# One DMA queue in a fixed order for the loads and stores of a weighted token copy

## The chip, the cores and the metric

The kernel runs on one core of a Trainium2 chip. The metric is the device time of that core in microseconds, as a median over runs. The profile is one execution recorded by the hardware profiler; its span, from the first to the last instruction, is about 2 us shorter than the device time.

## The reference

Every token vector of 512 floats is repeated k = 2 times, once for each of its two experts, and each copy is multiplied by that expert's weight. The expert indices are an input but are not used.

```
x:       (16, 1024, 512)  float32      33.55 MB
weights: (16, 1024, 2)    float32       0.13 MB
x_expanded = x[:, :, np.newaxis, :].repeat(k, axis=2)
out = x_expanded * weights[..., np.newaxis]     # (16, 1024, 2, 512)  67.11 MB
```

One multiplication for each float written: 33.69 MB are read and 67.11 MB are written.

## The kernel before, in words

The 16,384 tokens are laid over the 128 partitions, 128 consecutive tokens to a partition (A_TOTAL = 128). In both memory layouts one partition's share is contiguous, so a tile of 16 tokens is one run of 32 KB per partition, and so is an output tile of 8 tokens with two copies each. Every such transfer is 4096 KB.

The outer loop (L47) runs over 8 input tiles of TX = 16 tokens. It takes a buffer of x_pool, which has two, and loads the tile with a DMA issued from the Scalar engine (L49). The inner loop (L52) makes two output tiles of TO = 8 tokens from it, in buffers of o_pool, which has four. For each token and each k, VectorE multiplies 128x512 floats by a per-partition weight (L59), 16 instructions to an output tile and 32 to an input tile. A DMA issued from the Sync engine stores the output tile (L67). The weights are loaded once at the start from the Sync engine (L45). The two pools together take 2 x 32 KB + 4 x 32 KB = 192 KB of each partition.

The order of the work follows from three things. Each engine runs its own instructions in the order of the program. DMAs of the Sync engine go into one queue (q1 in the profile) and those of the Scalar engine into another (q10); both queues are served by the same 16 DMA engines. And the framework inserts the waits that the buffers need: a multiply waits until its input tile has landed and until the store that last used its output buffer has landed; a store waits for its 16 multiplies; a load waits for the 32 multiplies that read the buffer before. So the Scalar engine issues a load as soon as a buffer is free, whatever the stores are doing, and loads and stores share the DMA engines as they come.

Of the kernel before, what the change touches and what calls it, by code (L numbers as in the profile page):

```python
# [1 line left out]

# [4 lines left out]


@with_exitstack
def kernel(  # L10
    ctx: ExitStack,
    tc: tile.TileContext,
    x: bass.AP,
    expert_indices: bass.AP,
    expert_weights: bass.AP,
    out: bass.AP,
):
    nc = tc.nc

    batch, seq, hidden = x.shape  # L20
    k = expert_weights.shape[-1]
    P = nc.NUM_PARTITIONS
    ntok = batch * seq
    assert ntok % P == 0
    A_TOTAL = ntok // P

    xr = x.rearrange("b s h -> (b s) h").rearrange("(p a) h -> p (a h)", a=A_TOTAL)
    outr = out.rearrange("b s k h -> (b s) (k h)").rearrange(
        "(p a) n -> p (a n)", a=A_TOTAL
    )  # L30
    wr = expert_weights.rearrange("b s k -> (b s) k").rearrange(
        "(p a) k -> p (a k)", a=A_TOTAL
    )
    f32 = mybir.dt.float32
    row = k * hidden

    TX = 16
    TO = 8

    w_pool = ctx.enter_context(tc.tile_pool(name="w_pool", bufs=1))  # L40
    x_pool = ctx.enter_context(tc.tile_pool(name="x_pool", bufs=2))
    o_pool = ctx.enter_context(tc.tile_pool(name="o_pool", bufs=4))

    w_tile = w_pool.tile([P, A_TOTAL * k], f32)
    nc.sync.dma_start(out=w_tile, in_=wr)  # L45

    for i in range(A_TOTAL // TX):  # L47
        x_tile = x_pool.tile([P, TX * hidden], f32)
        nc.scalar.dma_start(  # L49
            out=x_tile, in_=xr[:, i * TX * hidden : (i + 1) * TX * hidden]  # L50
        )
        for j in range(TX // TO):  # L52
            o_tile = o_pool.tile([P, TO * row], f32)
            for t in range(TO):
                at = (j * TO + t) * hidden
                for kk in range(k):
                    c = (i * TX + j * TO + t) * k + kk
                    o = t * row + kk * hidden
                    nc.vector.tensor_scalar(  # L59
                        out=o_tile[:, o : o + hidden],  # L60
                        in0=x_tile[:, at : at + hidden],
                        scalar1=w_tile[:, c : c + 1],
                        scalar2=None,
                        op0=mybir.AluOpType.mult,
                    )
            first = (i * TX + j * TO) * row
            nc.sync.dma_start(out=outr[:, first : first + TO * row], in_=o_tile)  # L67


# [1 line left out]
_INS = ['x', 'expert_indices', 'expert_weights']  # L71
_OUTS = [((16, 1024, 2, 512), 'float32')]


# [23 lines left out]
```

## Time and profile before

| what | value |
|---|---|
| device time, median of 3 runs | 241.06 us (240.87 to 241.54) |
| span of the profiled execution | 238.8 us |
| VectorE busy | 102.5 us (43%), 256 multiplies |
| bytes moved | 100.81 MB, mean 422 GB/s |
| stores: 16 of 4096 KB | 44.9 us from issue to landing (median) |
| loads: 8 of 4096 KB | 23.9 us from issue to landing (median) |

How to read it: time from issue to landing includes the time in which a transfer stands in line behind others, so 44.9 us is no measure of the transfer itself. The share of DMA busy time is a mean over the 16 engines; in short windows it can exceed 1, since a packet is put to the window by its recorded times. Multiplies overlap a little, so that their mean duration (480 ns) is longer than the distance from one to the next (about 400 ns).

### The profile page before, as it was taken

The page shows a single profiled execution, that of the slowest core. Times are in us where ns is not written, and L with a number is a line of the kernel's source. Part 1 is how long each engine was busy: PE and PEld are TensorE (multiplying, and loading weights), DVE is VectorE, ACT ScalarE, POOL GpSimd, SP SyncE. Part 2 cuts the span into 40 slices and gives each one's busy share as a digit, 9 for nine tenths or more (in the row PEclk, how much of TensorE's full clock was granted, in tenths as well). Part 3 has the DMA queues.
Part 4 walks back from the last instruction along what each step waited for, and adds up shares of the span by engine and source line. Part 5 has one row for each costly group of instructions (what it writes and reads, how often), then busy time and mean ns, then how long its engine had stood idle before and what let it go on. Part 6 is the DMA issues. An engine that isn't in the chain of part 4 may idle for free.

```text
span 238.8 us, 358 instructions
## 1 busy us (share of the span) xinstructions
DVE 102.5 (43%) x256; POOL 0.2 (0%) x4
## 2 busy tenths in 40 slices
DVE  0079994059701904682054910739008486400000
POOL 0000000000000000000000000000000000000000
DMA  7999999999999999999999999999999999999994
GB/s 277 447 439 417 434 380 417 439 439 439 423 423 428 439 423 412 439 439 439 439 439 434 434 439 439 412 435 428 428 423 434 434 439 439 439 439 434 434 439 214
DMA packets 3602, 100.81 MB, mean 422 GB/s; under 512 B 400, under 2 KB 528, under 8 KB 528
## 3 DMA queue, kind: packets, MB, share of 16 engines
q1 hardware_dynamic: 2448, 67.24, 65.4%
q10 hardware_dynamic: 1152, 33.55, 33.2%
q14 instruction: 2, 0.02, 0.0%
HBM read 33.69 MB, written 67.11 MB: 422 GB/s over the span
## 4 chain that ended last, share of the span: by engine, by line
DMA 62%; DVE 18%; another core or an unknown queue 5%; DVEq 0%; issue 0%
DMA out_dram<-o_tile 57%; DVE o_tile L59 18%; DMA x_tile<-in_x_dram 5%; DVEq L93 0%; DVEq L59 0%
## 5 line engine op out<-in xcount | busy, mean ns | idle before, releaser
L59 DVE TENSOR_SCALAR o_tile<-x_tile,w_tile 128x512 f32<-128x512 f32 x256 | 102.5, 480 | 103.3 <-DMA out_dram<-o_tile 74.1
L82 POOL MEMSET const-bfloat16-1.0<- 128x1 bf16 x1 | 0.1, 101 | 0.0
L82 POOL MEMSET const-uint8-127<- 128x1 uint8 x1 | 0.1, 101 | 0.0
L82 POOL MEMSET const-float32-0.0<- 128x1 f32 x1 | 0.1, 98 | 0.2 <-issue 0.2
L82 POOL MEMSET const-float32-1.0<- 128x1 f32 x1 | 0.1, 98 | 0.0
## 6 DMA issues: line engine op xcount, KB each, us to landing
out_dram<-o_tile SPq DMA_DIRECT2D x16, 4096.0 KB, 44.9
x_tile<-in_x_dram ACTq DMA_DIRECT2D x8, 4096.0 KB, 23.9
w_tile<-in_expert_weights_dram SPq DMA_DIRECT2D x1, 128.0 KB, 10.1
```

What stands on the lines that cost most here:

```text
L59: nc.vector.tensor_scalar(out=o_tile[:, o : o + hidden], in0=x_tile[:, at : at + hidden], scalar1=w_tile[:, c : c + 1], scalar2=None, op0= ...
L82: nc = _bacc.Bacc("TRN2", target_bir_lowering=False, num_devices=1)
```

## The change

All big transfers go through the Sync engine's queue in a fixed order. Two input tiles are loaded first; then each round stores the two output tiles of tile i and after that loads tile i+2. The weights go to the Scalar engine's queue. Tiles, pools and multiplies stay as they were. The aim is that loads and stores don't share the DMA engines as chance has it, but in an order in which a load can't get ahead of, or slow down, the stores that free output buffers.

```
-    nc.sync.dma_start(out=w_tile, in_=wr)
+    nc.scalar.dma_start(out=w_tile, in_=wr)

-    for i in range(A_TOTAL // TX):
-        x_tile = x_pool.tile([P, TX * hidden], f32)
-        nc.scalar.dma_start(
-            out=x_tile, in_=xr[:, i * TX * hidden : (i + 1) * TX * hidden]
+    x_tiles = {}
+
+    def load(i):
+        x_tiles[i] = x_pool.tile([P, TX * hidden], f32, name="x_tile")
+        nc.sync.dma_start(
+            out=x_tiles[i], in_=xr[:, i * TX * hidden : (i + 1) * TX * hidden]
         )
+
+    load(0)
+    load(1)
+    for i in range(n_tiles):
+        x_tile = x_tiles.pop(i)
         for j in range(TX // TO):
...
             first = (i * TX + j * TO) * row
             nc.sync.dma_start(out=outr[:, first : first + TO * row], in_=o_tile)
+        if i + 2 < n_tiles:
+            load(i + 2)
```

More of the change, by code (lines that the diff above doesn't have):

```diff
@@ L38 @@
     TO = 8
+    n_tiles = A_TOTAL // TX
     w_pool = ctx.enter_context(tc.tile_pool(name="w_pool", bufs=1))
```

## The prediction

> **What bounds the kernel now.** I read the page's busy shares first, then the DMA queues, then a table of stretches, then the waits.
>
> The first view is the page's top: busy time, and the span in 40 slices.
>
> ```profile
> DVE 102.5 (43%) x256; POOL 0.2 (0%) x4
> DMA  7999999999999999999999999999999999999994
> GB/s 277 447 439 417 434 380 417 439 439 439 423 423 428 439 423 412 439 439 439 439 439 434 434 439 439 412 435 428 428 423 434 434 439 439 439 439 434 434 439 214
> q1 hardware_dynamic: 2448, 67.24, 65.4%
> q10 hardware_dynamic: 1152, 33.55, 33.2%
> ```
>
> The only computing engine works 43% of the span. The DMA row is 9 in every slice but the first and the last. The two queues, stores on q1 and loads on q10, add up to 98.6% of 16 engines' span. So the DMA engines are the bound, and what they don't fill is a head and a tail.
>
> The second view cuts the span where the mix of traffic changes. Columns: stretch, its length, DVE busy, POOL busy, clock, DMA share, GB/s.
>
> ```profile
> 0.00:2.00 2.00, 0.00 (x0) 0.20 (x4) 1.00 0.09 11
> 2.00:20.00 18.00, 6.69 (x17) 0.00 (x0) 1.00 1.03 438
> 20.00:50.00 30.00, 18.74 (x48) 0.00 (x0) 1.00 1.01 419
> 50.00:180.00 130.00, 58.02 (x145) 0.00 (x0) 1.00 1.00 431
> 180.00:235.00 55.00, 19.07 (x48) 0.00 (x0) 1.00 1.00 433
> 235.00:238.80 3.80, 0.00 (x0) 0.00 (x0) 1.00 0.30 129
> ```
>
> 2 to 20 us holds almost only loads, 180 to 235 us only stores (the queue rows of those stretches give 101.4% to q10 and 100.2% to q1). Between them both queues are at work. The DMA share is 1 throughout: the change can only gain by a higher rate at full DMA, by a shorter head or by a shorter tail. The rates are 438 (loads), 433 (stores) and 419 and 431 (both).
>
> The third view is who waits for whom.
>
> ```profile
> DVE o_tile L59 <- DMA out_dram<-o_tile: 74.1, 10, 12.9
> DVE o_tile L59 <- DMA x_tile<-in_x_dram: 25.3, 2, 13.3
> ```
>
> VectorE waits 74.1 us for stores to free one of the four output buffers. That looks like a stall to be cured, and the chain of work puts 57% of the span on stores. But while VectorE waits the DMA engines are full, so these waits cost nothing by themselves.
>
> **What the Trainium skill says.** (1) "DMA: Bandwidth & Descriptors", section "Issuing engines are not separate DMA queues": transfers issued from Sync and Scalar run on the same 16 engines, and several issuers save only issue time. The trace agrees: the two queues together reach 431 GB/s, stores alone 433. Issue time is small here (332 ns a store, 366 ns a load, 24 of them). (2) The same page, "Queues, rings and completion order": an engine takes turns between the queues that have work, at packet granularity, and within one queue takes descriptors in ring order. The trace agrees roughly: from 135 to 145 us each queue has 48.5% to 48.6%. (3) The same page, "Two DMAs through the same engine are not ordered": within a queue descriptors start in order but are pipelined. Stores alone show it: transfer follows transfer on one queue at 433 GB/s with no dent. (4) "Perfetto Trace Analysis", section "DMA Optimizations", advises the opposite of this change: inputs on one issuing engine, outputs on another, for more dynamic spread. No run here shows that the spread is worth anything when the engines are full.
>
> **The change part by part.**
>
> *The weights move to the Scalar queue, the first load to Sync.* Both were issued within 0.01 us of each other (0.72 and 0.73 us) and still are. One 128 KB and one 4096 KB transfer share the engines at the start as before. Cost 0.
>
> *What must be ready when.* All 24 big transfers now run in the order load 0, load 1, then (store 2k, store 2k+1, load k+2) six times, then four stores. A transfer is 4096 KB = 4.19 MB; at 433 GB/s it takes 9.7 us. A multiply is issued every 6.42/16 = 0.40 us, so a half tile (16) takes 6.4 us and a tile 12.8 us. Load 0 landed at 13.3 us by the first multiply, so store 0 may go at 19.8 us, as it does now; load 1 keeps the engines until about 22. Store 1 is ready at 26.3 and has its turn at about 32. Load 2 waits for tile 0's multiplies (26.1) and has its turn at about 41. Stores 2 and 3 are ready at 32.6 and 38.9, wanted at 51 and 61. From then on the rule is this: tile i+2 is multiplied in the 12.8 us after its load lands, and in that time the queue still holds two stores and a load, 3 x 9.7 = 29 us of work. Its four-deep output pool is no hindrance, as stores 2i and 2i+1 precede load i+2 in the queue and have landed when it does. At the end load 7 is followed by stores 12 and 13, 19.4 us, and store 14 needs 6.4. The tightest place is store 0, with 2 us in hand. So I expect no idle DMA anywhere.
>
> *The added waits.* A load now sits on Sync behind two stores and may hold the stores behind it. It waits for the multiplies of the tile two before, and the store just ahead of it has waited for the last of these already. So it adds no wait. The output stores behind it are wanted 10 to 30 us later. Cost 0.
>
> *What is left is the rate.* Head and tail stay: the bytes sum to 7.88 + 12.56 + 56.08 + 23.79 MB in 233 us and 0.49 MB after (1.1 us at 433), so the stream takes 234.1 us and head and tail 238.8 - 234.1 = 4.7 us. In the new order each engine sees long runs of one direction. Two ways to price that. If everything after 20 us runs at the store rate of 433, the 12.56 MB of 20 to 50 us take 29.0 us in place of 30, and the 56.08 MB of 50 to 180 us take 129.5 in place of 130: 1.5 us saved. If loads also keep their 438, the first stretch (4.82 MB loads, 7.73 MB stores) takes 11.0 + 17.9 = 28.9 us and the second (20.97 and 35.10 MB) 47.9 + 81.1 = 129.0: 1.1 + 1.0 = 2.1 us saved. I take the middle, 1.8 us.
>
> *The unknown: a change of direction within one queue.* The trace of before has none. There are 13 (load to store seven times, store to load six times). Lower bound: 0, since with both queues at work an engine changes direction at nearly every 1.2 us packet and still gives 431. Upper bound: a full start-up each time. The page "DMA: Bandwidth & Descriptors", section "Latency and other measured facts", gives about 0.6 us to the first byte on this path; 13 x 0.6 = 7.8 us as an estimate. I take 0, because stores follow each other on one queue without a dent.
>
> Sum: 241.06 - 1.8 = 239.2 us.
>
> **The rivals.**
>
> A, the forecast: the mixed stretches rise to the rate of unmixed ones; 239.2 us, between 238.9 and 239.6.
>
> B, no difference: 419 to 438 is scatter of the engines and not of the mix. For it: five-microsecond windows of stores alone go from 419 to 446, and the 130 us of mixed traffic lie only 0.5% under stores alone. The low 20 to 50 us stretch would then be a start-up matter that comes again. Time 240.5 to 241.5.
>
> C, slower: each change of direction in the one queue drains the engine, because there is no second queue with work to fill the gap. For it: the trace has never shown the case, and today a second queue covers whatever gap there is. Against it: transfers on one queue already join without a gap. At 0.3 us each it costs 13 x 0.3 = 3.9 us, less 1.8 us gained: 243.2 us; at the upper bound 247.1.
>
> D, a larger gain: long runs of one direction are better for the memory than the trace can show, and all runs at what loads alone had from 5 to 20 us, (444 + 446 + 433)/3 = 441. 100.81 MB / 441 GB/s = 228.6 us in place of 234.1: 5.5 us saved, 235.5 us. Against it: stores alone have 55 us to show such a rate and stay at 433.
>
> **How the numbers follow.** A 0.55, B 0.20, C 0.17, D 0.08. The time is A's. The range goes down to 237.0, half way to D and a bit over, since loads at 441 would bring nearly that, and up to 241.7, which takes in B and a small C; what is left out is most of C and most of D, about 0.2. Faster by over 0.3% (under 240.3): A and D, 0.63. Within 0.3%: B, 0.20. Slower: C, 0.17.
>
> **What the profile after would show.** Right: DMA digit 9 through all slices but the ends; one queue with about 98% of 16 engines; no stretch of 30 us under 430 GB/s, the one from 20 to 50 us above all; VectorE's waits now put down to loads, in six gaps of about 16 us (29.1 less 12.8), none of which costs anything. Wrong: digits of 7 or 8 that come back every 10 to 20 us, at the seams of loads and stores, for C; the same 419 from 20 to 50 us for B; 440 and over throughout for D. A DMA gap at 20 to 26 us would say that store 0 or 1 came too late for its turn.

## The result and the profile after

The changed kernel takes 244.87 us (244.36 to 245.54, 6 runs) against 241.08 us for the kernel before on the same chip: a ratio of 1.015, 95% interval 1.0121 to 1.0178. It is slower by 1.5%, and the forecast was 239.2 us. On a second chip, beside other kernels below, the ratio was 1.0089 (1.0058 to 1.012): there the changed kernel took much the same time, 245.12 us, and the kernel before took longer, 242.87 us. The kernel before was profiled only once, on the first chip, in an execution of 240.5 us.

The top of the page after, in the same lines as were shown of before:

```profile
DVE 102.0 (42%) x256; POOL 0.2 (0%) x4
DMA  6999999999999999999999999999999999999992
GB/s 276 433 434 426 431 432 410 404 372 437 431 431 426 372 431 431 431 426 415 431 431 431 431 420 427 442 431 431 426 431 431 431 431 431 431 437 431 437 431 108
q1 hardware_dynamic: 3456, 100.66, 97.6%
q10 hardware_dynamic: 144, 0.13, 0.2%
```

Between its ends the DMA row is as full as before, on one queue now. So the DMA engines don't wait for work. But the row of rates has dents (410, 404, 372, then 372 again, 415) that come back at a distance of about five slices, some 30 us, and grow shallower. The same stretches as before, columns as there:

```profile
20.00:50.00 30.00, 18.88 (x48) 0.00 (x0) 1.00 1.01 418
50.00:180.00 130.00, 56.21 (x142) 0.00 (x0) 1.00 1.00 424
180.00:235.00 55.00, 20.33 (x52) 0.00 (x0) 1.00 1.00 431
235.00:243.20 8.20, 0.00 (x0) 0.00 (x0) 1.00 0.46 200
```

The long middle fell from 431 to 424 GB/s at a DMA share of 1.00, which alone is 2.1 us. After 235 us there are 8.2 us in place of 3.8; that is no longer tail of itself, since all that was lost before comes out behind a fixed cut. A busy share of 1 with a lower rate says that the packets themselves take longer. To see which, here are stretches cut at the mean times at which the trace has one transfer end and the next begin: the store before load 2, load 2, two stores, load 3, two stores, load 4.

```profile
32.20:42.20 10.00, 6.67 (x17) 0.00 (x0) 1.00 1.01 419
42.20:53.20 11.00, 0.00 (x0) 0.00 (x0) 1.00 0.99 381
53.20:72.60 19.40, 12.76 (x32) 0.00 (x0) 1.00 1.00 431
72.60:83.40 10.80, 0.00 (x0) 0.00 (x0) 1.00 0.99 382
83.40:102.80 19.40, 12.76 (x32) 0.00 (x0) 1.00 1.00 432
102.80:112.80 10.00, 0.00 (x0) 0.00 (x0) 1.00 1.02 426
```

Loads 2 and 3 take 11.0 and 10.8 us, a store 9.7. The trace keeps every packet's duration, and they tell it best. A 32 KB packet takes 1213 ns in nearly all cases, in either direction and in both kernels: that is 27 GB/s an engine and 432 GB/s for 16. Call what a packet takes beyond that its stretch. The trace doesn't name the engine of a packet, but in most places a packet starts 3 to 4 ns before another one ends, and linked in this way the packets form 16 chains, taken here as the 16 engines. Mean duration in ns of the eight packets that each engine moves for a transfer, in order:

```
changed kernel  store 1  1213 1213 1213 1213 1213 1213 1236 1501
                load 2   1295 1470 1353 1318 1213 1213 1544 1583
                store 2  1213 1213 1213 1213 1213 1213 1213 1213
                store 3  1213 1213 1213 1213 1213 1213 1214 1247
                load 3   1229 1339 1246 1334 1213 1213 1689 1583
                store 4  1213 1213 1213 1213 1213 1213 1213 1213
                load 7   1213 1213 1213 1213 1213 1213 1225 1213
```

The stretch sits where the direction changes: in the last packet of the store ahead of a load, in the first four packets of the load and in its last two. The middle of the load and the stores behind it are at the minimum. It fades: the change from store 1 to load 2 costs 1.6 us, and load 7 has next to none.

In the kernel before each chain has 192 packets, eight for each of the 24 transfers, and so it is in the changed kernel, but for a few that can't be told apart, though the engines end 4 us apart there. So no engine takes over work from a late one. The time is then the minimum, plus the mean stretch, plus how much later than the mean the slowest engine ends. What is left after taking off both is the same within 0.3 us in these three profiles, and most of the rest of this document uses that sum:

```
                          mean stretch   slowest over mean   span    span less both
before                       1.66             1.03           238.8       236.1
changed                      4.25             2.86           243.2       236.1
changed, second chip         3.63             2.99           242.5       235.9
```

So of the 4.4 us between the two spans 2.6 are stretch and 1.8 are more uneven ends (the engines finish their last store 4.3 us apart, before 1.7). This compares one profile with one profile.

### The profile page after: what moved, and what is told of

It is laid out like the page before. It is cut to its first block, busy times and chain, and to the rows that moved or that the text cites. A ratio compares the mean times of both kernels' runs of the same rounds, so it can differ in the third digit from the quotient of the medians.

```text
span 243.2 us, 350 instructions
## 1 busy us (share of the span) xinstructions
DVE 102.0 (42%) x256; POOL 0.2 (0%) x4
## 4 chain that ended last, share of the span: by engine, by line
DMA 65%; DVE 22%; SPq 1%; issue 0%; DVEq 0%
DMA x_tile<-in_x_dram 60%; DVE o_tile L68 22%; DMA w_tile<-in_expert_weights_dram 5%; SPq L76 1%; DVEq L104 0%; DVEq L68 0%; SPq L52 0%
```

## The experiments

**Fewer changes of direction.** Four stores, then two loads: 7 changes in place of 13.

```
-        if i + 2 < n_tiles:
-            load(i + 2)
+        if i % 2 == 1 and i + 1 < n_tiles:
+            load(i + 1)
+            load(i + 2)
```

> One queue, but four stores and then two loads, so that the queue changes direction 7 times and not 13; all tiles as in the changed kernel. Theory (a change of direction costs, as all 16 engines make it at about the same time; in the changed kernel the loads and the packets at the seams took 3.9 us more than their minimum in the mean over the engines, and the engines ended 4.3 us apart): about 7/13 of the loss, 242 to 243 us. Rival 1 (one queue costs something by itself, whatever the order): 244.9 us again. Rival 2 (loads are slow when nothing but loads runs on all engines): 244.9 us or more, the load steps again 10 to 11 us against 9.7.

Measured: 242.02 us, 0.9971 (0.9952 to 0.999) of the kernel before. Since this was another chip than that of the first result, it was run again beside the changed kernel.

> Four stores then two loads, on the same chip as the changed kernel. Theory: 0.985 to 0.992 times the changed kernel, level with the kernel before, about 2.4 us of stretch. Rival (the chip of the earlier set was another, and the order makes no difference): the same as the changed kernel within 0.3%.

> The changed kernel again, beside the others of this set on one chip. Theory and rivals alike: 1.012 to 1.018 times the kernel before, and in the trace about 4 us of packets longer than their minimum in the mean over the engines, most of it at the ends of stores, and in loads, of the first 120 us.

Measured: pairs 242.89 us, 1.0002 (0.9981 to 1.0023) of the kernel before; changed 245.12 us, 1.0089 (1.0058 to 1.012). So pairs take 0.991 of the changed kernel and are level with the kernel before, as the theory had it. Two parts of the expectations missed: the changed kernel came out under its 1.012 to 1.018, and pairs had 3.3 us of stretch in this run, not 2.4. The stretches of the first pairs run: two stores, the store before load 2, load 2, load 3, two stores.

```profile
32.00:51.40 19.40, 6.97 (x18) 0.00 (x0) 1.00 1.00 432
51.40:61.30 9.90, 0.00 (x0) 0.00 (x0) 1.00 0.99 414
61.30:71.50 10.20, 0.00 (x0) 0.00 (x0) 1.00 0.99 414
71.50:81.20 9.70, 8.10 (x21) 0.00 (x0) 1.00 1.00 432
81.20:100.60 19.40, 17.33 (x44) 0.00 (x0) 1.00 1.01 434
```

Load 3 follows load 2 with nothing but loads on all engines and takes 9.7 us: loads as such are not slow (rival 2 falls), and nor is one queue as such (rival 1 falls). The three changes from stores to loads stretch packets by 0.68, 0.77 and 0.55 us; those from loads to stores by 0.08 the first time and by 0.00 the three later times. The ends are 1.5 us apart.

**More changes, smaller transfers.** Half and quarter size, buffers doubled and quadrupled.

```
-    TX = 16
-    TO = 8
+    TX = 8       # quarters: 4
+    TO = 4       # quarters: 2
+    NB = 4       # quarters: 8; loads ahead, bufs=NB and bufs=2 * NB
```

> One queue, two stores then one load, all transfers half as large (2 MB, 16 KB a partition) with twice the buffers, so 26 or so changes of direction. Theory, if each change costs the same: twice the loss, near 249 us; if the loss fades as the engines drift apart, 245 to 247. Rival 1 (the queue by itself): 244.9. Rival 2 (loads alone are slow): 244.9, as the bytes loaded are the same.

> As the kernel with halves, with transfers of 1 MB (8 KB a partition), four times the changes of direction. Theory, each change at the same cost: near 256 us; if a change costs only while some buffering in the DMA engine lasts, less, since the mix then comes close to that of two queues, which took turns packet by packet: 241 to 247. Rivals 1 and 2: 244.9.

Measured: 246.22 us, 1.0152 (1.0101 to 1.0202), and 248.0 us, 1.0222 (1.0178 to 1.0265). The mean stretch was 4.29 and 2.41 us, the ends 4.6 and 5.8 us apart. So the cost does not go with the number of changes: half the stretch of halves comes before 40 us, and it fades from there. The minimum grew: a 16 KB packet takes 611 ns and an 8 KB packet 309. Records of neighbours overlap by 3 to 4 ns, so what counts is the distance from one start to the next, 607 and 306 ns against 1209 for 32 KB; over all packets that is about 1.0 and 2.9 us more. With quarters the slowest engine also ended 4.4 us after the mean (2.9 in the changed kernel). Both together put them above the 241 to 247 us expected of a fading cost, although they have less stretch. The expectation that each change costs the same is refuted; "fades as the engines drift apart" fits, but no run shows that drift is the cause of the fading.

**Staggered engines.** Extra loads, never read, ahead of all others, to put some engines 1.2 to 3.6 us behind. The first version used neighbouring partitions, the second spread ones.

```
+    for n in (8, 4, 2):
+        skew = o_pool.tile([P, TO * row], f32, name="o_tile")
+        far = P // n       # second version; first: rows [:n]
+        nc.sync.dma_start(out=skew[::far, :], in_=xr[::far, 0 : TO * row])
     load(0)
```

> The changed kernel with three extra loads ahead of all others (into output buffers, never read) that use the first 8, the first 4 and the first 2 DMA engines, 32 KB an engine each, so that engines start 0, 1.2, 2.4 or 3.6 us late. Theory (the loss comes from all engines changing direction together): loads 2 and 3 take about 9.7 to 10.1 us in the mean in place of 11.0 and 10.8, and the time is 244.9 + 3.6 less most of 3.9 of stretch and 2.8 of uneven ends: 242 to 245. Rivals 1 and 2, and a cost per engine that doesn't depend on the others: the same 3.9 us of stretch, 246 to 248.5.

> The stagger again, with the rows of the extra loads spread over the partitions (every 16th, 32nd and 64th), as the earlier ones, on partitions next to each other, took 3.7 us in place of 1.2 and left the engines 10 us apart. Engines now start 0, 1.2, 2.4 or 3.6 us late. Theory: changes of direction no longer fall together, loads 2 and 3 take 9.7 to 10.1 us in place of 11.0 and 10.8, stretch under 2 us, time 243 to 246 although the last engines start 3.6 us late. Rival (a fixed cost per change on each engine): stretch 4 us as before, 247 to 248.5.

Measured: 255.94 us, 1.0548 (1.0503 to 1.0593), and 252.91 us, 1.0418 (1.038 to 1.0456). Neither made the stagger it was to make. Load 0 itself was stretched (packets took up to 4.6 us in the first version; all packets up to 22 us lost 6.0 and 3.0 us in the mean), and landed so late that store 0 missed its turn. The engines stood idle for about 2 us between 26 and 32 us, in the fifth slice of the DMA rows, first and second version:

```profile
DMA  7999599999999999999999999999999999999992
DMA  6999899999999999999999999999999999999992
```

That wait put them in step again: load 0 ended 5.1 and 4.4 us apart on the first and the last engine, store 0 only 1.6 and 1.7. From there on packets were stretched by 4.9 and 4.8 us, with no wide stagger to help or hinder. So these two kernels decide nothing about stagger.

**More mixing from the start, two queues.** The kernel before with three input and three output buffers (bufs=3 in both pools).

> The kernel before, two queues, with three input and three output buffers in place of two and four: load 2 stands ready from the start, so that when the first stores come the engines take turns between the queues packet by packet, in place of changing all to stores and then all to loads between 20 and 38 us. Theory: the stretch of the kernel before (1.7 us) falls under 1 us and the time by 0.5 to 1.5 us, ratio 0.994 to 0.998. Rival (the dip of the kernel before from 20 to 40 us is only a start-up matter, or the two queues' own): no change, or slower if three output buffers leave the queue empty.

Measured: 245.05 us, 1.0086 (1.0052 to 1.0121): the theory's forecast is wrong. The mix of loads and stores that starts at 20 us dents the rate:

```profile
20.00:30.00 10.00, 10.00 (x26) 0.00 (x0) 1.00 0.98 380
30.00:40.00 10.00, 2.58 (x7) 0.00 (x0) 1.00 1.00 433
40.00:50.00 10.00, 5.53 (x14) 0.00 (x0) 1.00 1.03 427
50.00:60.00 10.00, 0.89 (x3) 0.00 (x0) 1.00 1.02 426
60.00:70.00 10.00, 5.14 (x13) 0.00 (x0) 1.00 0.97 397
```

From 30 to 40 us the mix runs at 433, but from 40 to 75 us, with both queues at equal shares (50.7% and 49.7%), it has 1.3 us of stretch again. The mean stretch was 3.94 us and the ends 5.7 us apart, as much as in the changed kernel. So one queue isn't needed for the loss. Nor is a change from one mix to another: the kernel before went from the mix to stores alone and back three times between 85 and 165 us, with 0.15 us of stretch. Why the mix costs here and not there is not shown.

**Other addresses.** In all kernels so far a partition has 128 tokens, so rows lie 256 KB apart in x and 512 KB apart in the output. Here it has 127, and the last 128 tokens go one to a partition.

```
+    A = A_TOTAL - 1
...
-    xr = x.rearrange("b s h -> (b s) h").rearrange("(p a) h -> p (a h)", a=A_TOTAL)
+    xr = xt[: P * A, :].rearrange("(p a) h -> p (a h)", a=A)
...
+        if n < TX * hidden:
+            nc.sync.dma_start(out=x_tiles[i][:, n:], in_=xt[P * A :, :])
```

> The changed kernel with another mapping of tokens to partitions: 127 consecutive tokens each (rows of x 254 KB apart and rows of the output 508 KB apart, in place of 256 and 512), and the last 128 tokens one to a partition, in one small load and one small store. Theory (engines in step meet in the same part of the memory, as all their addresses lie a multiple of 256 KB apart, and each change of direction makes them sort themselves out anew): with other distances the stretch falls under 1.5 us and the time to 241 to 242, level with the kernel before. Rival (the change of direction itself costs, at whatever addresses): stretch about 4 us and 244.5 to 246, the small transfers adding up to 0.5.

> The kernel before with the same other mapping. Theory of addresses: its 1.7 us of stretch fall under 1 us, ratio 0.993 to 0.998. Rival: no change, 1.000 to 1.003.

> Pairs with 127 tokens a partition. With the changed kernel that mapping took the stretch after the start from 3.1 to 3.9 us to 1.4. Theory of addresses: stretch after the start 1 us or less in place of 2.2 to 2.7, ratio 0.993 to 0.998 to the kernel before. Rival (the mapping only moves the stretch between engines, or the ends are as uneven as with the changed kernel, 4.7 us): ratio 1.000 or more.

Measured: changed with 127, 244.35 us, 1.0065 (1.0044 to 1.0087), not the 241 to 242 expected; before with 127, 243.03 us, 0.9978 (0.9951 to 1.0006), no clear change; pairs with 127, 242.21 us, 0.9974 (0.9955 to 0.9994). The stretch, in the mean over the engines and in us, each row from one profile (the three with 127 tokens on other chips than the rest):

```
                      first 8 us   after     ends apart
before                   0.28       1.38        1.7
before, 127              0.74       1.02        3.7
changed                  0.33       3.93        4.3
changed, second chip     0.51       3.11        4.5
changed, 127             1.11       1.40        4.9
pairs                    0.25       2.15        1.5
pairs, again             0.61       2.66        1.7
pairs, 127               1.06       0.88        1.7
```

With the other distances the stretch after the start is less than half, with both orders in one queue. The kernel before had little to lose there; it fell to 1.02, and its total rose, where under 1 was expected. In the stretch of load 2, from 42.2 to 53.2 us, the changed kernel moved 381 GB/s; with 127 tokens the same stretch of time holds

```profile
42.20:53.20 11.00, 0.00 (x0) 0.00 (x0) 1.00 1.01 420
```

The change from store 1 to load 2 stretches packets by 0.45 us there, against 1.60 in the changed kernel, and it finds the engines as far apart in both: 1.4 us from the first to the last at the end of store 1. So the width of the stagger isn't what helps, and the stretch depends on where the rows lie in memory. The time gained little, as the ends stayed 4.9 us apart and the start lost 0.6 to 0.8 us.

**When a transfer is issued.** With pairs, a store after loads was ready about 2 us before its turn (its tile was loaded just before) and cost nothing; in the changed kernel stores stood ready much longer, and the ends of the loads ahead of them were stretched. Two kernels move this. In the first, half-size transfers, eight stores and four loads, let the store be ready early:

```
-        if i + NB < n_tiles:
-            load(i + NB)
+        if i % NB == NB - 1 and i + 1 < n_tiles:
+            for n in range(i + 1, i + 1 + NB):
+                load(n)
```

> Half-size transfers in the order of the kernel with pairs: eight stores, then four loads, so the same bytes between changes of direction and the same 7 changes, but the first store after the loads is ready some 11 us before its turn in place of 3. In the changed kernel the last two packets of a load before a store were 0.33 to 0.48 us longer; with pairs they were not. Theory a (a store that stands ready early is begun by the engines while they still load): the ends of the loads are stretched by 0.5 us or more, time 244 to 245.5. Theory b (a run of two loads lets the engines settle): no stretch at the ends of the loads, time 242.9 plus about 1.2 for the smaller packets (611 ns for 16 KB against 1213 for 32), 243 to 244.5.

Measured: 244.43 us, 1.0065 (1.004 to 1.009). The first store is issued at 11.8 us for a turn at about 23, the first of the second group at 72.1 for one at about 83:

```profile
11.79 13.00 SPq L77 DMA_DIRECT2D out_dram<-o_tile  x5
...
72.14 13.00 SPq L77 DMA_DIRECT2D out_dram<-o_tile  x5
```

The last load of each group is stretched by 1.26, 0.45, 0.13 and 0.42 us, nearly all of it in its last four packets, where pairs had 0.08 and then 0.00 three times. The early stores are the likely cause (theory a), though transfer size differs as well.

In the second, the other way round, loads are issued late: the last store before them is cut in four, with three small buffers, so that its end, and with it the loads behind it, can't be issued sooner.

```
+            last = i % 2 == 1 and j == 1 and i + 1 < n_tiles
+            part = 2 if last else TO
...
+                    o_tile = s_pool.tile([P, part * row], f32, name="s_tile")
```

> Four stores then two loads, but the fourth store of each group is cut in four pieces of 1 MB from a pool of three small buffers, so that its last piece can be multiplied and issued only when the first piece has landed; the loads, issued after it, so stand ready 4 to 5 us before their turn in place of some 20. Theory (a transfer of the other direction that stands ready early is begun too soon and stretches what goes before it): the stretch at the three changes from stores to loads, 0.6 to 0.9 us each with pairs, falls under 0.3, total stretch 1 to 1.6 us in place of 2.4 to 3.3, ratio 0.990 to 0.997 although the pieces' packets (309 ns for 8 KB) add some 0.6 us. Rival (the change from stores to loads costs by itself, whenever the load was issued): 0.6 to 0.9 us each again, ratio 1.000 to 1.005.

Measured: 241.83 us, 0.9969 (0.9952 to 0.9987). Loads 2 and 3 are issued at 57.1 us, 4 to 5 us before their turn, against 39.4 with pairs:

```profile
55.00 1.67 DVE L75 TENSOR_SCALAR s_tile<-x_tile,w_tile 128x512 f32<-128x512 f32 x4 [17.75 <-DMA out_dram<-s_tile]
56.70 0.33 SPq L83 DMA_DIRECT2D out_dram<-s_tile  x1
57.09 1.90 SPq L53 DMA_DIRECT2D x_tile<-in_x_dram  x2
```

The three changes from stores to loads stretch by 0.41, 0.30 and 0.53 us, where pairs had 0.68, 0.77, 0.55 and, run again, 0.90, 0.60, 0.79, and pairs with 127 tokens 0.12, 0.28, 0.10. Less, but not the under 0.3 that the theory asked for: how early the load stands ready is at most a part of it. The total was 2.2 us, where 1 to 1.6 was expected. Pairs with 127 tokens say the same, as their loads were issued at 40.1 us, as early as those of pairs, and cost least of all.

## Why the prediction was wrong

**What bounds the kernel, and what must be ready when: right.** The DMA engines are full throughout, and no store or load missed its turn. VectorE's waits changed as foretold, six gaps of 15.8 to 17.8 us behind loads (the view puts two of them down to "issue"), and cost nothing:

```profile
DVE o_tile L68 <- DMA x_tile<-in_x_dram: 66.3, 4, 17.5
DVE o_tile L68 <- issue: 34.9, 2, 17.8
```

**The weights on the other queue and the added waits: right,** at next to no cost: the weights now landed last, and the first multiply began at 13.45 us against 13.31.

**"What is left is the rate": wrong.** The step took mixed traffic (431 and 419) to be slower than unmixed (433, and 438 for loads). In the kernel before, of the 1711 packets of 32 KB between 50 and 180 us, mostly with both queues at work, 10 took over 1260 ns, and the mean was 1215 ns against 1213 for stores alone. There was nothing to gain there: the stretch in it was 0.18 us. The 438 of loads from 2 to 20 us was a window effect: the share printed beside it was 1.03, and a packet at its minimum gives 432. The rates had to be divided by their shares before they were compared. The gain of 1.8 us was worked out from rates that were not. Only the stretch from 20 to 50 us had a real loss, about 1.2 us, where the first stores and loads meet.

**The price of a change of direction, taken as 0: wrong, and the main error.** The stretch after the first 8 us was 3.93 us in the changed kernel, or 0.30 us for each of 13 changes in the mean, inside the bounds of 0 and 0.6. That this is just rival C's example is luck: the changes cost from 1.6 us down to nothing, and C's picture doesn't fit. An engine stood idle between packets for 0.07 us in all, in the mean; the packets' own records grew longer, and not only the first after a change but the last before it too. So the DMA digits stayed at 9, where C was to show 7 or 8: a busy share can't show a stretched packet, and the rate can. The reason given for 0, that stores follow each other on one queue without a dent, says nothing of a change of direction. The lower bound leaned on the mixed stretch of the kernel before, which did run without loss; 20 to 38 us of the same profile, where loads and stores first met, had 1.2 us of stretch and was the warning. The kernel with three buffers shows that even a steady mix can be stretched.

**The sum had no term for uneven engines: wrong.** It took the mean rate for the time. But each engine has a fixed share of the bytes, so the slowest sets the end: 1.8 us more than before.

**Rival C** was the case that came, at 0.17; its 243.2 us still counted the gain of 1.8 and had no uneven ends. **Rival B** had the low stretch from 20 to 50 us right, which came again (418). **D** is out: the long run of stores from 180 to 235 us moved 431 GB/s, no more than before. Its 441 was a window effect too, of shares 1.03, 1.03 and 1.00.

**What stays open.** That the stretch depends on the order of the transfers and on addresses is shown; that an early store takes part is likely. How the engines or the memory produce it isn't shown. The Trainium skill, "DMA: Bandwidth & Descriptors", section "Latency and other measured facts", reports rows at large powers of two slowing copies down and a padded distance curing it, and takes streams in step for the cause as an inference. For 512 KB, the distance of our output rows, it gives 207 GB/s per direction for copies within HBM, close to the 214 that it calls full; our stores at that distance ran at 432, in one direction. So no lasting slowdown is stated or seen at our distances, but the stretch at changes does fall when the distance isn't a power of two. That early transfers matter would fit that page's section "Two DMAs through the same engine are not ordered", where reading and writing in an engine are separate queues and descriptors are pipelined; no run here separates reading from writing. Why the ends are 3.5 to 5.8 us apart in some kernels and 1.5 to 1.8 in others with similar stretch is open too, and so is how much stretch the kernel before has in its longer executions, which were not profiled.

## What to carry to other kernels

When the DMA engines are full and the packets already take their minimum, an order of transfers has no rate to win and can lose: compare packet durations, or rates divided by shares, before you forecast a gain from the order. If loads and stores share a queue, try few changes of direction: here four stores and two loads were level with two free queues, two and one 0.9 to 1.5% behind. The number of changes isn't all, as the same seven with half-size transfers and early stores were 0.65% behind. The time is that of the slowest engine, so count the spread of the ends as well as the mean. Versions slightly better than both (late, pairs with 127 tokens, and one run of pairs) gained 0.3%, so little was left to win by the order.

## What had not been expected of the hardware

A 32 KB packet takes 1213 ns in nearly all cases, loading or storing, and in the kernel before also when two queues take turns. From one start to the next it is 1209 ns, for 16 KB 607 and for 8 KB 306, so smaller rows cost 0.4% and 1.2% of rate by themselves. Loads of few rows ahead of a full one, as in the staggered kernels, delayed the full one by far more than their bytes: 14 packets added, about 1 us an engine, and packets up to 22 us were stretched by 6.0 and 3.0 us; the idle time before store 0 came on top.
